# S5 scan states laid out in runs of two blocks, with a 17th row for the carry

## Chip, core and metric

The kernel runs on one core of one Trainium2 chip. The metric is device time in microseconds (us) of one execution; a single number for a kernel is the median of its runs.

## What is computed

The program is two trunk layers of a diffusion backbone over 2048 latent tokens and 256 context tokens, with 1024 channels. The change is in the second (odd) layer, in its bidirectional S5 branch: 512 channels in 32 groups of 16, each group with 64 complex states and two directions.

```python
def linear_scan(lam_bar, bu, h0, reverse):
    """h_t = lam_bar * h_{t-1} + bu_t along axis 1 (or reversed)."""

def s5_direction(u_lat, u_ctx, ...):          # context scan first, the latent scan starts from its end
    h_ctx = linear_scan(lam_bar, drive(u_ctx), None, reverse)
    h_end = h_ctx[:, 0] if reverse else h_ctx[:, -1]
    h_lat = linear_scan(lam_bar, drive(u_lat), h_end, reverse)
    return read(h_lat), ...

z = gelu(y_forward + y_backward + d_skip * u);  val, gt = split(z @ w_glu + b_glu);  out = val * sigmoid(gt)
```

Beside it the odd layer has a gated MLP branch: layer norm, a 128 x 128 mix of positions, and two gates, with its own input projections.

## The kernel before

Eight tokens are folded into one position by matrices computed ahead, so that the scan runs over 288 positions a direction: 32 of the context and 256 of the latent tokens. `middle` projects the input `u` of the branch band by band, copies it out of PSUM with ScalarE into `s` (L1430) and stores it in DRAM as `s_d`.

`s5_quarter` (L1617) then runs four times, each time for 8 of the 32 groups (below: a quarter). Its parts:

- **Drive.** For each of four group pairs `gp`, the position table `mi` and the input `U` are loaded, TensorE writes `pd` (L1634), and ScalarE copies it to the state tile `S` (L1636): 128 partitions x (2 directions, 2 parts (real, imaginary), 4 pairs, 288 positions), fp32.
- **Scan in blocks.** The 288 positions are 18 blocks of 16. VectorE steps through the 16 rows of all blocks at once: 15 steps of five instructions (L1655 to L1660), each step reading row i-1 and updating row i of 18 blocks, both directions and 8 part-and-pair rows. Three instructions have 288 elements a partition and two have 144. Neighbouring elements of a row are 16 floats (64 bytes) apart, since a block's positions are contiguous.
- **Carries.** 17 more steps of the same five lines, on 16 or 8 elements, take the last state of each block to the next.
- **Correction.** The carry, multiplied by the powers of the eigenvalue in the table `pa`, is added to the other 15 rows of 17 blocks: the forward direction on VectorE in 8 instructions of 1020 elements, the backward direction on POOL in 16 of 510 (L1697 to L1700 for both).
- **Output.** SyncE's queue brings `S` to `O` in another partition order (L1710). TensorE sums three matmuls a group (L1718 to L1720); ScalarE applies GELU (L1722), VectorE notes the maximum (L1723), and `z` goes to DRAM.

`S` has two buffers, `O` three. In program order the four quarters come first and then `odd_pair`, once for every 256 latent tokens, for the gated MLP; a compile-time planner orders the instructions of each engine by its own times, and so the pairs' work lies between that of the quarters. Each engine works off its list in order. In a pair, TensorE fills up to four PSUM banks `pu` (L181), and VectorE takes them: the layer-norm statistics of the first two (L1576), a row of small instructions for a reciprocal square root (L122 to L136), a gate (L1594) for the third and fourth, and a product (L1598). POOL multiplies `vc` (L1588) and `sy` (L1607). With all banks full, TensorE waits until VectorE gets to the gate.

After the quarters and six pairs come `glu_in`, `glu_z` and two further pairs, then `glu` (product `yg`, L1780) and `final` (the output projection).

Of the kernel before, what the change touches and what calls it, by code (L numbers as in the profile page):

```python
# [9 lines left out]
F32 = mybir.dt.float32  # L10
# [3 lines left out]
AF = mybir.ActivationFunctionType  # L14
OP = mybir.AluOpType
# [39 lines left out]
class Kern:  # L55
# [729 lines left out]
    def step(self):  # L785
        c = next(self.steps, (7, 0))
        if isinstance(c, tuple):
            self.ahead = c
        else:
            self.ahead = None  # L790
            self.credit = max(self.credit - c, -AHEAD)
# [573 lines left out]
    def middle(self, mw, w2, ow):  # L1365
        nc, I, tc = self.nc, self.I, self.tc
# [3 lines left out]
        gp = {k: self.gate_row(self.wop, k) for k in ("l0", "c0")}  # L1370
        ws = self.load_w(w2, I["w_in_odd"], 2560, 1536, 512)
        u_s = self.product(self.u_h, ws[2], 1.0)
# [9 lines left out]
        with self.pool_("midh", side="right") as pool:  # L1382
            for at, b in enumerate(MID_ORDER):
# [40 lines left out]
                if b == 3:  # L1424
                    mw.close()
                    self.s5a = mw.enter_context(self.pool_("s5a"))
                for j in range(4):
                    s = pool.tile([128, 8, n // 8], F32, name=self.name("s"), tag="s", bufs=1)
                    ps = self.mid_mm(ws, j, hs, n)
                    nc.scalar.activation(s.rearrange("p s n -> p n s"), ps.rearrange("p (n s) -> p n s", s=8), AF.Copy,  # L1430
                                         scale=u_s)
                    for at in ([32 + t0 // 8] if b < 4 else [0, 288]):
                        nc.sync.dma_start(self.s_d[j, :, :, at:at + n // 8], s)
                if b == 3:
# [182 lines left out]
    def s5_quarter(self, pool, pb, j):  # L1617
        nc = self.nc
        pa = pool.tile([128, 2, 2, 2, 4, 17], F32, name=self.name("pa"), tag="pa", bufs=2)
        nc.sync.dma_start(pa, self.pa_d[:, j].rearrange("p (a d r g i) -> p a d r g i", a=2, d=2, r=2, g=4))  # L1620

        S = pb.tile([128, 2, 2, 4, 288], F32, name=self.name("S"), tag="S", bufs=2)
        for gp in range(4):
            mi = pool.tile([128, 512], F32, name=self.name("mi"), tag="mi", bufs=2)
            nc.sync.dma_start(mi, self.min_d[4 * j + gp])
            U = pool.tile([128, 2, 320], F32, name=self.name("U"), tag="U", bufs=2)
            for gpar in range(2):
                nc.sync.dma_start(U[:, gpar, :], self.s_rows(j, 2 * gp + gpar, 0, 320))
            for d in range(2):
                ps = self.ps.tile([128, 2, 512], F32, name=self.name("pd"), tag="s", bufs=1)  # L1630
                for ri in range(2):
                    for gpar in range(2):
                        c = (2 * d + ri) * 128 + 64 * gpar
                        nc.tensor.matmul(ps[64 * gpar:64 * gpar + 64, ri, 0:288], mi[:, c:c + 64],  # L1634
                                         U[:, gpar, 32 * d:32 * d + 288], start=True, stop=True)
                nc.scalar.activation(S[:, d, :, gp, :], ps[:, :, 0:288], AF.Copy)  # L1636
        DS, RS = 8 * 288, 4 * 288
        t1 = pool.tile([128, 4 * 17 * 15], F32, name=self.name("t1"), tag="t1", bufs=1)
        t2 = pool.tile([128, 4 * 17 * 15], F32, name=self.name("t2"), tag="t2", bufs=1)

        def ap(off, dstep, n, step):
            return bass.AP(tensor=S.tensor, offset=S.offset + off, ap=[list(S.ap[0]), [dstep, 2], [288, 8], [step, n]])

        def half(off, dstep, n, step):
            return bass.AP(tensor=S.tensor, offset=S.offset + off, ap=[list(S.ap[0]), [dstep, 2], [288, 4], [step, n]])

        def tab(part):
            return pa[:, part]

        def step(cur, prev, ar, ai, n):  # L1650

            m = 16 * n
            x1 = t1[:, 0:m].rearrange("p (d q n) -> p d q n", d=2, q=8)
            x2 = t2[:, 0:m].rearrange("p (d q n) -> p d q n", d=2, q=8)
            nc.vector.tensor_tensor(x1, ap(*prev), ar, op=OP.mult)  # L1655
            nc.vector.tensor_tensor(x2, ap(*prev), ai, op=OP.mult)  # L1656
            nc.vector.tensor_tensor(ap(*cur), ap(*cur), x1, op=OP.add)  # L1657
            nc.vector.tensor_tensor(half(*cur), half(*cur), x2[:, :, 4:8], op=OP.subtract)  # L1658
            c2 = (cur[0] + RS,) + cur[1:]
            nc.vector.tensor_tensor(half(*c2), half(*c2), x2[:, :, 0:4], op=OP.add)  # L1660

        ar = [tab(p)[:, :, :, :, 16].rearrange("p d r g -> p d (r g)")[:, :, :, None].to_broadcast([128, 2, 8, 18])
              for p in range(2)]
        for i in range(1, 16):
            step((i, DS + 15 - 2 * i, 18, 16), (i - 1, DS + 17 - 2 * i, 18, 16), ar[0], ar[1], 18)
        a16 = [tab(p).rearrange("p d r g i -> p d (r g) i") for p in range(2)]

        def last(p):

# [1 line left out]
            return bass.AP(tensor=x.tensor, offset=x.offset + 15, ap=[list(x.ap[0]), [8 * 17 - 15, 2], [17, 8], [1, 1]])  # L1671

        ll = [last(0), last(1)]
        for k in range(1, 18):
            step((16 * k + 15, DS + (17 - k) * 16 - (16 * k + 15), 1, 1),
                 (16 * k - 1, DS + (18 - k) * 16 - (16 * k - 1), 1, 1), ll[0], ll[1], 1)
        for d in range(2):

            cur0 = d * DS + (16 if d == 0 else 1)
            car0 = d * DS + (15 if d == 0 else 16)  # L1680

            def v(off, q, i):
                return bass.AP(tensor=S.tensor, offset=S.offset + off,
                               ap=[list(S.ap[0]), [288, q], [16, 17], [1, 15] if i else [0, 15]])

            i0 = 0 if d == 0 else 1
            tb = [a16[p][:, d, :, None, i0:i0 + 15].to_broadcast([128, 8, 17, 15]) for p in range(2)]
            eng, m = (nc.vector, 4) if d == 0 else (nc.gpsimd, 2)
            if d == 0:
                x1, x2 = t1, t2  # L1690
            else:
                x1, x2 = [pool.tile([128, m * 17 * 15], F32, name=self.name("tp"), tag=f"tp{k}", bufs=1) for k in range(2)]
            x1, x2 = [x.rearrange("p (q b i) -> p q b i", q=m, b=17) for x in (x1, x2)]
            for ri in range(2):
                for q in range(0, 4, m):
                    cur = v(cur0 + ri * RS + q * 288, m, True)
                    eng.tensor_tensor(x1, v(car0 + ri * RS + q * 288, m, False), tb[0][:, q:q + m], op=OP.mult)  # L1697
                    eng.tensor_tensor(x2, v(car0 + (1 - ri) * RS + q * 288, m, False), tb[1][:, q:q + m], op=OP.mult)
                    eng.tensor_tensor(cur, cur, x1, op=OP.add)
                    eng.tensor_tensor(cur, cur, x2, op=OP.add if ri else OP.subtract)  # L1700
        T = pool.tile([128, 8, 128], F32, name=self.name("T"), tag="T", bufs=1)
# [2 lines left out]
                                                        [[240, 16], [32 * 240, 8], [1, 128]]))  # L1704
        for gp in range(4):

            O = pb.tile([128, 2, 2, 288], F32, name=self.name("O"), tag="O", bufs=3)
            for gpar in range(2):
                for ri in range(2):
                    nc.sync.dma_start(O[64 * ri:64 * ri + 64, gpar], S[64 * gpar:64 * gpar + 64, :, ri, gp, :])  # L1710
            for gpar in range(2):
                g = 2 * gp + gpar
                u = pool.tile([128, 256], F32, name=self.name("Uy"), tag="Uy", bufs=3)
                nc.sync.dma_start(u, self.s_rows(j, g, 32, 256))
                mo = pool.tile([128, 2, 144], F32, name=self.name("mo"), tag="mo", bufs=3)
                nc.sync.dma_start(mo, dap(self.mo_d, (8 * j + g) * 256 * 144, [[144, 128], [128 * 144, 2], [1, 144]]))
                ps = self.psg((128, 256))
                nc.tensor.matmul(ps, T[:, g, :], u, start=True, stop=False)  # L1718
                nc.tensor.matmul(ps, mo[:, 0, 16:144], O[:, gpar, 0, 31:287], start=False, stop=False)
                nc.tensor.matmul(ps, mo[:, 1, 0:128], O[:, gpar, 1, 1:257], start=False, stop=True)  # L1720
                z = pool.tile([128, 256], F32, name=self.name("z"), tag="z", bufs=3)
                nc.scalar.activation(z, ps, AF.Gelu_apprx_tanh)  # L1722
                nc.vector.tensor_reduce(self.zmax[:, 8 * j + g:8 * j + g + 1], z, axis=AX.X, op=OP.max,  # L1723
                                        apply_absolute_value=True)
                nc.sync.dma_start(dap(self.z_d, (j * 128 + 16 * g) * 2048, [[256, 8], [2048, 16], [1, 256]]), z)
# [34 lines left out]
    def glu(self, pool, zs, z0):  # L1760
# [3 lines left out]
        for b in range(4):  # L1764
            zh, zl = self.glu_z(pool, zs, b) if b else z0
            for j in range(4):
# [4 lines left out]
                for i, w in ((1, wg[1]), (0, wg[0])):  # L1771
# [5 lines left out]
                nc.scalar.activation(va, ps[0], AF.Identity, bias=bv[:, j:j + 1], scale=uvc)  # L1777
                nc.vector.scalar_tensor_tensor(va, th, 1.0, va, op0=OP.add, op1=OP.mult)
                y = pool.tile([128, 512], F32, name=self.name("yg"), tag="yg", bufs=2)
                nc.vector.tensor_tensor(y.rearrange("p (n t) -> p t n", t=8), va.rearrange("p (t n) -> p t n", t=8),  # L1780
                                        G.rearrange("p (n t) -> p t n", t=8), op=OP.mult)
                self.note_max(y, b, 4 + j)
                nc.sync.dma_start(self.yo_d[4 + j, :, 512 * b:512 * b + 512], y)

# [86 lines left out]
```

## Time and profile before

| | us |
|---|---|
| median of 3 runs | 2462.55 |
| lowest, highest | 2454.91, 2464.0 |
| the profiled execution | 2459.69 |
| its span in the trace | 2457.9 |
| TensorE busy | 2223.6 |
| VectorE (DVE) busy | 1625.8 |
| ScalarE (ACT) busy | 1047.0 |
| GpSimd (POOL) busy | 445.7 |

The span leaves 1.8 us of the profiled execution outside; that execution is 2.9 us below the median. Shares over the whole span are averages over very different stages. The four quarters lie between about 1700 and 2090 us of the span, and the window table and the instruction timelines of this stretch are what to read.

### The profile page before, as it was taken

The numbers are of one execution on the slowest core, as the hardware profiler recorded it, in microseconds if no ns is written. First come the engines' busy times: TensorE is split into PE (matmuls) and PEld (weight loads), VectorE is DVE, ScalarE is ACT, GpSimd is POOL, SyncE is SP. The second block draws the span as 40 slices with busy tenths as digits, with TensorE's granted clock in tenths as the row PEclk, the third lists the DMA queues.
The fourth block names the chain that finished last, engine by engine and source line by source line (L and its number), as shares of the span: only waits on it lengthen the run. The fifth ranks groups of instructions, "written<-read, shape, count | busy, mean of one in ns | idle before, by whom it ended". The sixth has DMA issues, their size and how long they took to land.

```text
span 2457.9 us, 43136 instructions
## 1 busy us (share of the span) xinstructions
PE 2223.6 (90%) x15860; PEld 1421.2 (58%) x15860; DVE 1625.8 (66%) x4343; ACT 1047.0 (43%) x2208; POOL 445.7 (18%) x533
## 2 busy tenths in 40 slices
PE   5999997998999999999878999978968787999998
PEld 2667784675766666666564566666534443544443
DVE  5888413466576666766686767751799998457555
ACT  4822232455556565555565555532211211244232
POOL 0123100122222222222340000000053154110000
PEclk8999998999999999999988999989989888999999
DMA  9845756224343343523433435552234532556332
GB/s 321 255 119 147 192 166 177 69 74 135 83 139 99 93 140 102 138 76 102 155 113 102 164 124 138 163 175 91 79 87 124 143 98 79 147 151 206 116 116 90
DMA packets 344165, 324.98 MB, mean 132 GB/s; under 512 B 93154, under 2 KB 290158, under 8 KB 343058
## 3 DMA queue, kind: packets, MB, share of 16 engines
q1 hardware_dynamic: 343842, 322.20, 44.1%
q8 instruction: 125, 2.05, 0.3%
q14 instruction: 86, 0.70, 0.1%
q10 hardware_dynamic: 112, 0.03, 0.0%
HBM read 210.10 MB, written 102.59 MB: 127 GB/s over the span
## 4 chain that ended last, share of the span: by engine, by line
PE 60%; DVE 22%; DMA 8%; issue 3%; ACT 3%; SPq 2%; POOL 1%; DVEq 0%; ACTq 0%; POOLq 0%
PE pg L181 36%; PE pu L181 6%; PE S L997 4%; PE PT L1016 4%; DVE S L1657 2%; PE pv L1030 2%; DVE t L1655 2%; DVE t L1656 2%; DVE S L1658 2%; DVE wl L190 1%; PE pa L331 1%; DMA wf<-in_w_in_even_dram 1%; DVE S L1660 1%; PE pv L1033 1%; DMA s_d<-s 1%
## 5 line engine op out<-in xcount | busy, mean ns | idle before, releaser
L181 PEld LDWEIGHTS <-wh 128*128 128x128 f16 x2944 | 280.0, 98 | 168.3 <-issue 10.8
L1000 DVE CUSTOM_DVE_ANT_0 P<-S,bias,slab 128x640 f32<-128x640 f32 (+2 forms) x216 | 193.6, 896 | 162.6 <-PE S L997 161.5
L189 ACT ACTIVATE ph<-PT 128x384 f16<-128x384 f32 (+1 forms) x408 | 172.6, 457 | 217.2 <-PE PT L1016 216.2
L181 PE MATMUL pu<-wh,h1p 128*128 128x512 f16 x768 | 191.2, 397 | 45.0 <-DVE Gs L1594 42.5
L181 PEld LDWEIGHTS <-h1p 128*128 128x128 f16 x1152 | 115.2, 101 | 192.4 <-issue 72.9
L949 POOL TENSOR_TENSOR bias<-G,masks 128x384 f32<-128x384 f32 (+1 forms) x144 | 152.6, 1060 | 349.6 <-DVE t L1000 326.9
L181 PEld LDWEIGHTS <-wl 128*128 128x128 f16 x1472 | 142.7, 100 | 116.2 <-issue 31.9
L190 DVE SCALAR_TENSOR_TENSOR pl<-PT,ph 128x384 f16<-128x384 f32 (+1 forms) x408 | 195.1, 508 | 13.9 <-ACT ph L189 12.5
L1002 ACT ACTIVATE P<-P,t 128x640 f32<-128x640 f32 (+2 forms) x216 | 181.2, 839 | 40.2 <-DVE t L1000 38.9
L181 PE MATMUL pg<-hh,wl 128*128 128x512 f16 (+1 forms) x800 | 183.6, 363 | 15.6 <-DVE stg L190 7.5
L181 PE MATMUL pg<-hl,wh 128*128 128x512 f16 (+1 forms) x800 | 181.9, 361 | 0.0
L181 PE MATMUL pg<-hh,wh 128*128 128x512 f16 (+1 forms) x800 | 180.6, 358 | 0.0
L181 PEld LDWEIGHTS <-yh 128*128 128x128 f16 x1088 | 106.5, 98 | 124.3 <-issue 0.8
L1016 PE MATMUL PT<-ident,P 128*128 128x128 f32 x1104 | 162.8, 277 | 11.5 <-DVE pl L190 9.6
L997 PEld LDWEIGHTS <-Q 128*128 128x128 f16 x1776 | 132.7, 99 | 62.7 <-issue 22.0
L997 PE MATMUL S<-K,Q 128*128 128x128 f16 (+1 forms) x1776 | 160.2, 234 | 1.8 <-DVE t L1000 1.7
L181 PE MATMUL pg<-wh,yl 128*128 128x512 f16 x544 | 133.1, 386 | 5.2 <-DVE yl L190 5.1
L1016 PEld LDWEIGHTS PT<-ident,P 128*128 128x128 f32 x1104 | 120.6, 142 | 20.7 <-issue 8.4
L1037 POOL TENSOR_TENSOR o<-o 128x64 f32<-128x64 f32 x216 | 73.3, 339 | 323.9 <-ACT o L1036 322.6
L181 PE MATMUL pg<-wh,yh 128*128 128x512 f16 x544 | 130.3, 379 | 0.0
L181 PE MATMUL pg<-wl,yh 128*128 128x512 f16 x544 | 130.2, 379 | 0.0
L156 DVE TENSOR_REDUCE t<-wf 128x1 f32<-128x1024 f32 x68 | 82.5, 1216 | 71.9 <-DMA wf<-in_w_in_odd_dram 25.4
(341 smaller groups left out, 4168.3 us busy)
## 6 DMA issues: line engine op xcount, KB each, us to landing
wada<-in_w_ada_dram SPq DMA_DIRECT2D x34, 512.0 KB
x<-in_x_dram SPq DMA_DIRECT2D x32, 512.0 KB
wf<-in_w_in_even_dram SPq DMA_DIRECT2D x28, 512.0 KB
V<-vs SPq DMA_DIRECT2D x192, 64.0 KB
K<-kd SPq DMA_DIRECT2D x96, 128.0 KB
wf<-in_w_in_odd_dram SPq DMA_DIRECT2D x20, 512.0 KB
Y<-ys SPq DMA_DIRECT2D x144, 64.0 KB
O<-S SPq DMA_DIRECT2D x64, 144.0 KB
```

Source lines behind the costliest of these rows:

```text
L156: nc.vector.tensor_reduce(m[:, i:i + 1], f, axis=AX.X, op=OP.max, apply_absolute_value=True)
L181: nc.tensor.matmul(ps, a(k), b(k), start=(n == 0), stop=(n == 3 * kb - 1))
L189: nc.scalar.activation(hi, src, AF.Copy, scale=scale)
L190: nc.vector.scalar_tensor_tensor(lo, src, scale, hi, op0=OP.mult, op1=OP.subtract)
L949: nc.gpsimd.tensor_tensor(q4(bv), gv, q4(masks[:, m0:m0 + 128 * nch]), op=OP.add)
L997: nc.tensor.matmul(S[:, at:at + m], u["q"], K[:, hl, off:off + m], start=(hl == 1), stop=(hl == 0))
L1000: nc.vector.tensor_tensor_reduce(P[:, 0:n], S[:, 0:n], u["B"][:, 0:n], u["negf"], 3.4e38, OP.add, OP.min, nm)
L1002: nc.scalar.activation(P[:, 0:n], P[:, 0:n], AF.Exp, bias=nm, scale=-1.0, accum_out=l)
L1016: self.nc.tensor.transpose(PT[:, c - a:c - a + 128], P[:, c:c + 128], self.ident)
L1030: nc.tensor.matmul(pv, ph[:, i * 128:(i + 1) * 128], vals[i][:, hd * 128:hd * 128 + 128], start=(i == 0), stop=False, skip_group_check=True)
L1037: nc.gpsimd.tensor_tensor(o["t"][:, hd * 64:(hd + 1) * 64], o2[:, 0:64], o2[:, 64:128], op=OP.add)
L1655: nc.vector.tensor_tensor(x1, ap(*prev), ar, op=OP.mult)
```

## The change

- `S` grows from 288 to 306 floats a row. Two neighbouring blocks share a run: 9 runs of 34 floats, 17 rows of 2, with the position in row r of block k at 34 (k // 2) + 2 r + k % 2. Row 0 (forward) or row 16 (backward) holds the state carried into the block.
- A scan step then covers 9 pairs of neighbouring floats for each of its 16 part-and-direction rows, still 288 and 144 elements. There are still 15 steps.
- The carry steps write into the new row: 16 steps and one copy in place of 17. The first carry is zero, set by POOL in 16 elements a quarter.
- The correction covers 18 blocks: 1080 and 540 elements for 1020 and 510. The powers are doubled into a tile `tw` (one buffer) by one ScalarE instruction a quarter of 1024 elements.
- The output matmuls read the state before each position as 8 runs of 32 floats; `O` and its transfers grow with `S`.
- Positions are put in the new order when `s` is written, by two ScalarE instructions a band of 512 in place of one, and put back in `glu` by two VectorE instructions of 256 elements in place of one of 512.

```diff
-                    nc.scalar.activation(s.rearrange("p s n -> p n s"), ps.rearrange("p (n s) -> p n s", s=8), AF.Copy,
-                                         scale=u_s)
+                    sv = s.rearrange("p s (b i k) -> p b k i s", i=16, k=2)
+                    pv = ps.rearrange("p (b k i s) -> p b k i s", k=2, i=16, s=8)
+                    for h in range(n // 256):
+                        nc.scalar.activation(sv[:, h], pv[:, h], AF.Copy, scale=u_s)
...
-        S = pb.tile([128, 2, 2, 4, 288], F32, name=self.name("S"), tag="S", bufs=2)
+        NS = 9 * 34
+        DS, RS = 8 * NS, 4 * NS
+        S = pb.tile([128, 2, 2, 4, NS], F32, name=self.name("S"), tag="S", bufs=2)
+        nc.gpsimd.memset(bass.AP(tensor=S.tensor, offset=S.offset, ap=[list(S.ap[0]), [DS + 8 * 34 + 33, 2], [NS, 8], [1, 1]]), 0.0)
...
-                nc.scalar.activation(S[:, d, :, gp, :], ps[:, :, 0:288], AF.Copy)
+                nc.scalar.activation(S[:, d, :, gp, :].rearrange("p r (b x) -> p r b x", x=34)[:, :, :, 2 - 2 * d:34 - 2 * d],
+                                     ps[:, :, 0:288].rearrange("p r (b x) -> p r b x", x=32), AF.Copy)
+        tw = pool.tile([128, 2, 2, 8, 32], F32, name=self.name("tw"), tag="tw", bufs=1)
+        nc.scalar.activation(tw.rearrange("p a d q (i k) -> p (a d q) i k", k=2),
+                             pa.rearrange("p a d r g i -> p (a d r g) i")[:, :, 0:16, None].to_broadcast([128, 32, 16, 2]),
+                             AF.Copy)
...
-            return bass.AP(tensor=S.tensor, offset=S.offset + off, ap=[list(S.ap[0]), [dstep, 2], [288, 8], [step, n]])
+        def rows(r, q):
+            o, dstep = 2 * r, DS + 32 - 4 * r
+            return bass.AP(tensor=S.tensor, offset=S.offset + o, ap=[list(S.ap[0]), [dstep, 2], [NS, q], [34, 9], [1, 2]])
...
-        for i in range(1, 16):
-            step((i, DS + 15 - 2 * i, 18, 16), (i - 1, DS + 17 - 2 * i, 18, 16), ar[0], ar[1], 18)
+        for r in range(2, 17):
+            step(lambda q: rows(r, q), lambda q: rows(r, q), lambda q: rows(r - 1, q), ar[0], ar[1], (9, 2))
...
-        for k in range(1, 18):
-            step((16 * k + 15, DS + (17 - k) * 16 - (16 * k + 15), 1, 1),
-                 (16 * k - 1, DS + (18 - k) * 16 - (16 * k - 1), 1, 1), ll[0], ll[1], 1)
+        nc.vector.tensor_copy(one(0, 1, 8), one(16, 0, 8))
+        for k in range(1, 17):
+            step(lambda q: one(0, k + 1, q), lambda q: one(16, k, q), lambda q: one(0, k, q), ll[0], ll[1], (1,))
...
-                               ap=[list(S.ap[0]), [288, q], [16, 17], [1, 15] if i else [0, 15]])
+                if row is None:
+                    return bass.AP(tensor=S.tensor, offset=S.offset + o + 2, ap=[list(S.ap[0]), [NS, n], [34, 9], [2, 15], [1, 2]])
+                return bass.AP(tensor=S.tensor, offset=S.offset + o + 2 * row, ap=[list(S.ap[0]), [NS, n], [34, 9], [0, 15], [1, 2]])
...
-                nc.tensor.matmul(ps, mo[:, 0, 16:144], O[:, gpar, 0, 31:287], start=False, stop=False)
-                nc.tensor.matmul(ps, mo[:, 1, 0:128], O[:, gpar, 1, 1:257], start=False, stop=True)
+                nc.tensor.matmul(pv, mo[:, 0, 16:144], ov[:, 0, 1:9, 0:32], start=False, stop=False)
+                nc.tensor.matmul(pv, mo[:, 1, 0:128], ov[:, 1, 0:8, 2:34], start=False, stop=True)
...
-                nc.vector.tensor_tensor(y.rearrange("p (n t) -> p t n", t=8), va.rearrange("p (t n) -> p t n", t=8),
-                                        G.rearrange("p (n t) -> p t n", t=8), op=OP.mult)
+                for h in range(2):
+                    c = slice(256 * h, 256 * h + 256)
+                    f = lambda t: t[:, c].rearrange("p (k i t) -> p k i t", k=2, t=8)
+                    nc.vector.tensor_tensor(f(y), va.rearrange("p (t b i k) -> p b k i t", t=8, b=2, k=2)[:, h], f(G), op=OP.mult)
```

## Rows read from the trace of the kernel before

**Rows 1.** The page: busy us, share of the span and instructions of each engine.

```profile
PE 2223.6 (90%) x15860; PEld 1421.2 (58%) x15860; DVE 1625.8 (66%) x4343; ACT 1047.0 (43%) x2208; POOL 445.7 (18%) x533
```

**Rows 2.** Windows: stretch, length, busy us (instructions) by engine, TensorE clock, DMA, GB/s.

```profile
1735.00:1797.00 62.00, 60.84 (x363) 32.22 (x362) 59.55 (x182) 14.12 (x26) 6.22 (x5) 1.00 0.26 82
1797.00:1825.00 28.00, 11.13 (x42) 4.42 (x41) 28.00 (x26) 0.69 (x1) 27.15 (x16) 0.78 0.26 63
1825.00:1883.00 58.00, 54.28 (x307) 33.70 (x306) 55.95 (x180) 15.44 (x30) 5.55 (x4) 0.93 0.52 149
...
2080.00:2273.00 193.00, 189.59 (x914) 95.79 (x913) 114.51 (x221) 72.09 (x101) 23.77 (x19) 0.99 0.57 166
```

**Rows 3.** Waits of 1690 to 2110 us: waiter, releaser, us in total, times, longest.

```profile
PE pu L181 <- DVE Gs L1594: 42.5, 7, 11.1
```

**Rows 4.** The page's chain that ended last: shares of the span by line.

```profile
PE pg L181 36%; PE pu L181 6%; PE S L997 4%; PE PT L1016 4%; DVE S L1657 2%; PE pv L1030 2%; DVE t L1655 2%; DVE t L1656 2%; DVE S L1658 2%; DVE wl L190 1%; PE pa L331 1%; DMA wf<-in_w_in_even_dram 1%; DVE S L1660 1%; PE pv L1033 1%; DMA s_d<-s 1%
```

**Rows 5.** Groups by line and shape, 1690 to 2100 us: count, busy us, mean ns, idle before.

```profile
L1657 DVE TENSOR_TENSOR S<-S,t 128x288 f32<-128x288 f32 x60 | 45.9, 765 | 1.0
L1655 DVE TENSOR_TENSOR t<-S,pa 128x288 f32<-128x288 f32 x60 | 41.7, 695 | 1.5 <-ACT S L1636 0.3
L1656 DVE TENSOR_TENSOR t<-S,pa 128x288 f32<-128x288 f32 x60 | 40.7, 679 | 0.0
...
L1658 DVE TENSOR_TENSOR S<-S,t 128x144 f32<-128x144 f32 x60 | 31.1, 518 | 1.2
...
L1660 DVE TENSOR_TENSOR S<-S,t 128x144 f32<-128x144 f32 x60 | 24.0, 401 | 0.8
...
L1656 DVE TENSOR_TENSOR t<-S,pa 128x16 f32<-128x16 f32 x68 | 12.1, 178 | 0.0
```

**Rows 6.** Timeline of VectorE: one scan step and the next one's start; start, us.

```profile
1754.37 0.64 DVE L1655 TENSOR_TENSOR t<-S,pa 128x288 f32<-128x288 f32 x1
1754.92 0.63 DVE L1656 TENSOR_TENSOR t<-S,pa 128x288 f32<-128x288 f32 x1
1755.59 0.67 DVE L1657 TENSOR_TENSOR S<-S,t 128x288 f32<-128x288 f32 x1
1756.30 0.41 DVE L1658 TENSOR_TENSOR S<-S,t 128x144 f32<-128x144 f32 x1
1756.74 0.41 DVE L1660 TENSOR_TENSOR S<-S,t 128x144 f32<-128x144 f32 x1
1757.18 0.64 DVE L1655 TENSOR_TENSOR t<-S,pa 128x288 f32<-128x288 f32 x1
```

**Rows 7.** Line L1697: count, duration ns min/median/max, first and last start, shape.

```profile
L1697 POOL TENSOR_TENSOR tp<-S,pa x16: 1089/2062/2102, 1796.7 to 2082.7; 128x510 f32<-128x510 f32 x16
L1697 DVE TENSOR_TENSOR t<-S,pa x8: 1220/1702/2192, 1796.6 to 2066.4; 128x1020 f32<-128x1020 f32 x8
```

**Rows 8.** Timeline of VectorE: a scan instruction while POOL runs its correction.

```profile
1813.47 1.46 DVE L1655 TENSOR_TENSOR t<-S,pa 128x288 f32<-128x288 f32 x1
```

**Rows 9.** Timelines: TensorE's matmuls of a statistics bank, and VectorE's reading of that bank.

```profile
1783.38 3.62 PE L181 MATMUL pu<-wh,h1p 128*128 128x512 f16 x16
...
1793.83 0.69 DVE L1576 BATCH_NORM_STATS2 t<-pu 128x6 f32<-128x512 f32 x1
...
1869.40 3.62 PE L181 MATMUL pu<-wh,h1p 128*128 128x512 f16 x16
...
1878.44 0.69 DVE L1576 BATCH_NORM_STATS2 t<-pu 128x6 f32<-128x512 f32 x1
```

**Rows 10.** Lines L1430 and L1780: count, duration ns min/median/max, starts, shapes.

```profile
L1430 ACT ACTIVATE s<-pg,slab x20: 685/1143/1174, 1406.2 to 1653.2; 128x512 f32<-128x512 f32 x16, 128x256 f32<-128x256 f32 x4
...
L1780 DVE TENSOR_TENSOR yg<-va,Gd x16: 1077/1095/1102, 2192.5 to 2274.5; 128x512 f32<-128x512 f32 x16
```

**Rows 11.** Timelines of POOL and SyncE's queue: `sy`, and the last transfer out of `S`.

```profile
1841.55 2.80 POOL L1607 TENSOR_TENSOR sy<-sy,Gs 128x512 f32<-128x512 f32 x2 [5.23 <-ACT sy L1606]
...
1842.80 0.61 SPq L1710 DMA_DIRECT2D O<-S  x1
```

## What the change should do

> **What bounds the kernel now.** Read first the page's busy shares [rows 1]: TensorE has 90% of the span, VectorE 66%. By that alone a VectorE edit would seem worth little. Then read the windows of the S5 stretch [rows 2]. From 1735 to 1797 us VectorE is busy 59.55 of 62 us and TensorE 60.84; in the 28 us that follow, VectorE is busy throughout, POOL for 27.15, and TensorE for only 11.13, at a granted clock of 0.78; from 1825 to 1883 VectorE is busy again for 55.95 of 58. This pattern repeats, once a quarter, until about 2080, after which TensorE is the full engine (189.59 of 193). The waits say who holds whom: TensorE waited 42.5 us for the gate L1594 on VectorE, seven times [rows 3]. The chain agrees: the scan lines L1655 to L1660 hold about 9% of the span on it [rows 4], some 220 us. So for four quarters VectorE's list sets the pace, TensorE idles at the end of each quarter, and after 2080 TensorE has a fixed amount of work. What VectorE saves in the quarters is saved at the end, as far as TensorE keeps up.
>
> **The scan steps.** These are 60 steps of five instructions, 183.4 us busy in all [rows 5]. An undisturbed step is 0.64, 0.63 and 0.67 us for the instructions of 288 elements and 0.41 twice for those of 144; the next starts 2.81 us after it [rows 6]. What would they cost at the rate of contiguous data? The nearest rows are an instruction of 1020 elements, contiguous in its rows, at 1.220 us when nothing holds it [rows 7], and one of 16 at 0.178 [rows 5]. Between them lie 1.042 us for 1004 elements: 1.04 ns an element and 0.16 us fixed. So 288 elements would take 0.46 us and 144 would take 0.31. At 64 bytes' step they take (0.64 - 0.16) / 288 = 1.66 ns an element. A step thus saves 0.18 + 0.17 + 0.21 + 0.10 + 0.10 = 0.76 us, if pairs of neighbouring floats run at the contiguous rate; 60 steps save 45.6. No row shows an operand in runs of two, so the bounds are 0 (the strided row) and 45.6 (the contiguous one). I take 45.6: a run of two halves the jumps, and a strided element costs 1.6 times a contiguous one, so one jump in two elements fits into the time that the second element gives.
>
> [...] No row of this trace shows the pair.
>
> **Carries.** One step of five instructions goes and one copy comes. At 0.178 us each [rows 5], which overlap partly, that is 0.5 us a quarter, -2 in all; bounds 0 and -3.
>
> **The correction.** 60 more elements on VectorE add 0.06 us to each of 8 instructions; 30 more on POOL, at 1.089 us for 510, add 0.06 to each of 16 [rows 7]. The two slow each other: POOL's median is 2.06 us against a least of 1.09. POOL fills the window of 28 us and VectorE's work of this time goes through between its instructions, so the window grows by between 16 x 0.06 = 1.0 and 6% of 28 = 1.7 us. I take 1.2 a quarter: +5. In the first three quarters it lies between the statistics and the gate for which TensorE waits; in the last one POOL's `sy` is queued behind it.
>
> **What TensorE can follow.** The first bank of statistics was full half way through the row of 16 matmuls, at 1785.2, and VectorE read it at 1793.83; in the second quarter 1871.2 and 1878.44 [rows 9]. So the slack is 8.6 and 7.2 us. VectorE would arrive 15 x 0.76 + 0.5 = 11.9 us earlier in the first quarter, with TensorE full until then: VectorE waits some 3.2. In the second, some 13 steps lie behind the last gate, 10.4 us with the carries, but TensorE's own start moves with the gate and with `vc`; I take a wait of 1.8. In the last two quarters the same reading gives no slack under 10 us, and I take 0. Together +5; bounds 0 and +15 (a loss of some 3.5 in each of four).
>
> **On ScalarE, the queues and in `glu`.** `s`: a band of 512 goes from 1.143 us to two of 0.685 [rows 10], +0.23 us in 16 places; most lie under TensorE, the last four on a chain of copies and stores: +0.5, bounds 0 and +3.6. `tw`: at (1.143 - 0.685) / 256 = 1.8 ns an element, 1.9 us of ScalarE a quarter, which is busy 15.44 of 58 us there [rows 2]; it waits for POOL's correction of the quarter before, and behind it in ScalarE's list stand `S` copies, gates and `vc`, needed by TensorE. ScalarE is nearly empty in the correction window (0.69 of 28), so I take 0; without that cover it is 1.9 x 4 = 7.6. The memset: a rival, below. `O` transfers: 6% more bytes, 144 to 153 KB, same count, same place in SyncE's queue; 0. The three matmuls of a group read 32 contiguous floats at a time in place of 256; 0, since 9 runs have 8 more jumps in 256 elements. `yg`: 1.095 us becomes two of 256 elements, at 0.43 (contiguous) to 0.59 (strided) each: -0.2 to +0.1 in 16 places, while TensorE is full; 0, bounds -4 and +2.
>
> **The sum.** -45.6 - 2 + 5 + 5 + 0.5 = -37 us. The profiled execution has 2459.7, so it would come to 2422.6. It lies 2.9 below the median of the runs; against the median, 2462.55, the forecast is 2425. One caution on the size: of the scan's mean durations, 3.06 us a step against 2.76 undisturbed, 0.30 x 60 = 18 us are waits beside POOL [rows 5, 6]; I keep them, though shorter instructions may meet POOL less.
>
> **Rivals.**
>
> *Pairs run no faster (slower).* Every second element still jumps; if that is what costs, the steps save nothing, and the carry of the correction, which was one float repeated, becomes a pair repeated 15 times and pays too. With r ns an element for pairs, the steps save 60 x 1152 x (1.66 - r) ns; the correction's first two lines lose 17,280 x (r - 1.04) ns on VectorE and as much on POOL, which hold one another, and the rest costs about 3.5 us. The signs change at r = 1.42. At r = 1.66 it is +21 + 3.5, some 2487 us; with POOL's half hidden, 2476. For it: no row shows a pair. Against it: the strided rate is 1.6 and not 2 or more times the contiguous one. At r between 1.2 and 1.42 it would be 2438 to 2462.
>
> *TensorE or the order becomes the bound.* If all four quarters can give no more than the least slack, 7.2 us, the gain is 28.8 - 5 = 24 and the time 2439. For it: TensorE was full for 60.84 of 62 us in the first scan [rows 2]. Against it: 16.9 us of each 28 us window are idle on TensorE, and the banks wait for VectorE there.
>
> *POOL's list.* The memset of a quarter's `S` waits until the transfers out of the same buffer, two quarters earlier, are through. The last of them was issued at 1842.80, while POOL began `sy` at 1841.55 [rows 11]. A memset put ahead of `sy` in POOL's list holds `sy`, and the transposes behind it on TensorE, for 3 to 4 us; this can come in two quarters: +7, 2432.
>
> *The lock with POOL.* A scan instruction in the correction window takes 1.46 us in place of 0.64 [rows 8]: it waits for POOL's. Two of the steps in each of three quarters lie there; if they gain nothing, 3 x 2 x 0.76 = 4.6 us go, 2430. [...]
>
> *More than forecast.* Without VectorE's waits for TensorE, and with half of the 18 us beside POOL gone, it is 37 + 5 + 9 = 51 us: 2411.
>
> **How the numbers follow.** The forecast, with the two small rivals that lie beside it (2415 to 2436): 0.58. More: 0.10. TensorE as bound (2436 to 2450): 0.14. Pairs at a rate between (2438 to 2462): 0.09. Pairs no faster (2462 to 2487): 0.09. A range from 2406 to 2451 leaves out the last case, most of the one before and a little at the low end. A measurement of this kernel can tell about 0.5%, 12.3 us, from no change: below 2450.2 is faster, above 2474.9 slower. Faster: 0.58 + 0.10 + 0.13 + 0.02 = 0.83; same: 0.11; slower: 0.06.
>
> **What the profile would show.** Right: L1655's successor at 0.46 us undisturbed and its half-size companion at 0.31, a step of about 2.05 us, the corrections of neighbouring quarters some 10 us closer together, TensorE's wait for the gate still there but its idle time smaller, and the stretch after the quarters unchanged in length. Wrong: 0.64 us for the pairs; or 0.46 with VectorE idle for TensorE in front of the statistics; or a correction whose first two lines grow by more than 6%; or POOL or ScalarE standing at the memset or at `tw` with `sy` or a gate behind it.

## The result, and the profile after

The changed kernel takes **2587.99 us** in the median (2583.30 to 2592.68), the kernel before 2461.51 beside it. The ratio is 1.0518, with a 95% interval of 1.0490 to 1.0547: **slower by 126 us**. The forecast was 2425 us, with a range of 2406 to 2451.

The scan itself did what was forecast: it became faster. A timeline of VectorE in the changed kernel (start, us; an undisturbed step), to set beside [rows 6]:

```profile
1745.56 0.46 DVE L1677 TENSOR_TENSOR t<-S,pa 128x288 f32<-128x288 f32 x1
1745.94 0.45 DVE L1678 TENSOR_TENSOR t<-S,pa 128x288 f32<-128x288 f32 x1
1746.42 0.46 DVE L1679 TENSOR_TENSOR S<-S,t 128x288 f32<-128x288 f32 x1
1746.92 0.31 DVE L1680 TENSOR_TENSOR S<-S,t 128x144 f32<-128x144 f32 x1
1747.15 0.30 DVE L1682 TENSOR_TENSOR S<-S,t 128x144 f32<-128x144 f32 x1
1747.48 0.46 DVE L1677 TENSOR_TENSOR t<-S,pa 128x288 f32<-128x288 f32 x1
```

From one step to the next it is 1.92 us, where it was 2.81. VectorE is also less busy over the whole span, 1580.6 us where it was 1625.8 [rows 1]. The page of the changed kernel, busy time by engine, and then TensorE, VectorE and TensorE's clock in 40 slices of the span (tenths):

```profile
PE 2243.7 (87%) x15860; PEld 1431.6 (55%) x15860; DVE 1580.6 (61%) x4343; ACT 1050.1 (41%) x2228; POOL 445.9 (17%) x537
...
PE   5998998999999999998789999882442899999998
...
DVE  5888313665676766665867677339997122358555
...
PEclk8999999999999999998889999895666999999999
```

The hole is in slices 28 to 31, some 1750 to 2005 us: the S5 quarters. VectorE is full there and TensorE nearly idle; afterwards it is the other way round. The window view (stretch, length, busy us and instructions by engine, granted clock, DMA share, GB/s), of the changed kernel:

```profile
1740.00:2090.00 350.00, 175.21 (x734) 96.18 (x735) 257.51 (x714) 42.87 (x81) 115.48 (x72) 0.70 0.38 101
2090.00:2420.00 330.00, 327.27 (x1692) 168.71 (x1691) 148.58 (x337) 98.73 (x152) 34.29 (x26) 1.00 0.33 99
```

and of the kernel before:

```profile
1740.00:2090.00 350.00, 285.89 (x1468) 156.20 (x1465) 335.21 (x834) 63.24 (x125) 135.22 (x84) 0.90 0.37 103
2090.00:2420.00 330.00, 321.05 (x1519) 154.82 (x1517) 185.49 (x445) 115.58 (x157) 16.62 (x12) 0.99 0.47 144
```

Up to 2090 us TensorE has run half as many instructions as before, 734 for 1468, and been busy 110.7 us less. Who holds it? The waits of TensorE, 1690 to 2110 us (waiter, releaser, us in total, times, longest):

```profile
PE pg L1743 <- DMA O<-S: 117.3, 4, 48.5
```

The wait for the gate on VectorE, 42.5 us [rows 3], is gone. In its place TensorE waits four times, once a quarter, for the corrected states that the transfers bring to `O`: nothing else stands in its list that it could do meanwhile. What used to stand there is the gated MLP. The first instruction of a pair on ScalarE, the gate `G` (count, duration in ns, first and last start), in the changed kernel:

```profile
L1555 ACT ACTIVATE G<-pg,slab x8: 682/687/687, 2021.9 to 2145.8; 128x512 f32<-128x512 f32 x8
```

and before:

```profile
L1552 ACT ACTIVATE G<-pg,slab x8: 682/687/689, 1714.2 to 1951.3; 128x512 f32<-128x512 f32 x8
```

All eight came beside the quarters; now the first starts 308 us later, when the quarters are through. So the question was not what the scan costs but why the pairs no longer lie between the quarters.

**The theory: 2,176 bytes.** The planner lets an instruction that writes a buffer wait for the last reader of whatever held those bytes. S5's buffers are laid from one end of SBUF, those of the pairs (`G`, `vc`, `Gs`, `sy`, `syT`) from the other. `G` has the lowest address of these. In the two built programs (bytes of a partition):

```
                         before    after
last O buffer ends at    133,920   141,888
G begins at              139,712   139,712
room between them          5,792   - 2,176
```

The growth of 7,968 can be added up from the diff: `S` 2 x 16 x 18 x 4 = 2,304, `O` 3 x 4 x 18 x 4 = 864, `t1` and `t2` 480, the two `tp` 240, `tw` 4,096; that is 7,984, and rounding takes off 16. With it the third `O` buffer covers `G` and the first bytes of `vc`, and it is last read in the last quarter.

**The rivals** of this theory (A): (B) the scan's own new waits (the zeroing on POOL, `tw` with its one buffer, the larger states) push the pairs back; (C) the planner's order is so touchy that any shift of addresses or names upsets it.

### The profile page after: what moved, and what is told of

The parts are those of the page before. It is cut to its first block, busy times and chain, and to the rows that moved or that the text cites. A ratio compares the mean times of both kernels' runs of the same rounds, so it can differ in the third digit from the quotient of the medians.

```text
span 2586.9 us, 43210 instructions
## 1 busy us (share of the span) xinstructions
PE 2243.7 (87%) x15860; PEld 1431.6 (55%) x15860; DVE 1580.6 (61%) x4343; ACT 1050.1 (41%) x2228; POOL 445.9 (17%) x537
## 4 chain that ended last, share of the span: by engine, by line
PE 68%; DVE 13%; DMA 6%; issue 3%; POOL 3%; ACT 3%; SPq 1%; DVEq 0%; ACTq 0%; POOLq 0%
PE pg L181 37%; PE pu L181 12%; PE S L997 4%; PE PT L1016 4%; PE pv L1030 2%; DMA wf<-in_w_in_even_dram 1%; PE pa L331 1%; DVE t L1677 1%; PE pv L1033 1%; DVE S L1679 1%; DVE S L1680 1%; DVE t L1678 1%; DVE wl L190 1%; DVE t L156 1%; POOL tp L1720 1%
## 5 line engine op out<-in xcount | busy, mean ns | idle before, releaser
L181 PE MATMUL pu<-wh,h1p 128*128 128x512 f16 x768 | 176.9, 379 | 3.3 <-ACT vc L1590 1.7
L1743 PE MATMUL pg<-O,mo 128*128 128x256 f32 x64 | 26.5, 505 | 118.2 <-DMA O<-S 117.3
```

Source lines behind the costliest of these rows:

```text
L181: nc.tensor.matmul(ps, a(k), b(k), start=(n == 0), stop=(n == 3 * kb - 1))
L1743: nc.tensor.matmul(pv, mo[:, 0, 16:144], ov[:, 0, 1:9, 0:32], start=False, stop=False)
```

## The experiments

Medians are in us; each ratio is against runs of the kernel before on the same chip (2459.14 for the first four runs, 2464.77 for the next four, 2459.72 for two, 2463.45 for the last).

**1 and 2: only bytes, on the kernel before.** An unused tile ahead of `S`; the two runs differ by 32 bytes.

```diff
+        pad = pool.tile([128, 1448], F32, name=self.name("pad"), tag="pad", bufs=1)
         S = pb.tile([128, 2, 2, 4, 288], F32, name=self.name("S"), tag="S", bufs=2)
```

```diff
+        pad = pool.tile([128, 1456], F32, name=self.name("pad"), tag="pad", bufs=1)
         S = pb.tile([128, 2, 2, 4, 288], F32, name=self.name("S"), tag="S", bufs=2)
```

> The kernel before with one unused tile of 5,792 bytes per partition ahead of S in S5's buffers; nothing reads or writes it, and no instruction is added. Theory A (memory): S5's buffers and those of the pairs (G, vc, Gs, sy, syT) grow towards one another from the two sides of SBUF, 5,792 bytes were free between them before, and the change took 7,968; G then shares addresses with the third O buffer and no pair can begin before the last quarter. This pad uses the free bytes up exactly, nothing overlaps, so the time is that of before, 2455 to 2470 us, and G's first ScalarE instruction still stands near 1714 us. Theory B (the changed scan's own waits: the zeroing on GpSimd, the doubled powers with one buffer, the bigger scan state) has nothing to do with memory and expects 2455 to 2470 too. Theory C (any shift of addresses or of names makes the instructions be ordered otherwise) expects a time that differs, by tens of us, in either direction.

> As the run before, with an unused tile of 5,824 bytes, 32 bytes more: G and the third O buffer now share 32 bytes per partition. Theory A: the pairs wait for the last quarter as in the changed kernel, G's first ScalarE instruction moves from about 1714 us to behind 2050 us, TensorE stands idle beside the scans, and the time is above that of the changed kernel, since the scan is still the slow one: 2588 plus some 40 to 80 us (four quarters at 86.6 in place of 67 us), 2600 to 2680 us. Theory B: 2455 to 2470 us, for no part of the change is in it. Theory C: no telling, but no reason for a time that differs from the pad of 5,792 by over 100 us.

Measured: 2462.65 (ratio 1.0011, 0.9996 to 1.0025) and **2638.24** (1.0731, 1.0715 to 1.0747). Without any instruction of the change, 32 bytes cost 176 us. In the first the gate is where it was (count, ns, first and last start):

```profile
L1552 ACT ACTIVATE G<-pg,slab x8: 681/687/689, 1718.0 to 1954.9; 128x512 f32<-128x512 f32 x8
```

In the second, its instruction on VectorE (L1553, right behind it) first starts at 2070.5, and TensorE's costliest wait of 1690 to 2110 us is that of the changed kernel, and longer, since this kernel has the old, slower scan:

```profile
L1553 DVE SCALAR_TENSOR_TENSOR G<-G,pg x8: 686/688/689, 2070.5 to 2194.1; 128x512 f32<-128x512 f32 x8
```

```profile
PE pg L1720 <- DMA O<-S: 171.6, 4, 60.6
```

So B is not needed for the jump, since nothing of the changed scan is in this kernel; whether it adds to it, runs 3 and 4 tell. C falls: 5,792 bytes moved nothing, and the jump comes within the 32 bytes in which the two sets of buffers meet.

**3 and 4: the whole change, with room.** Fewer buffers elsewhere in S5, nothing else.

```diff
-                mo = pool.tile([128, 2, 144], F32, name=self.name("mo"), tag="mo", bufs=3)
+                mo = pool.tile([128, 2, 144], F32, name=self.name("mo"), tag="mo", bufs=2)
-                z = pool.tile([128, 256], F32, name=self.name("z"), tag="z", bufs=3)
+                z = pool.tile([128, 256], F32, name=self.name("z"), tag="z", bufs=2)
```

```diff
-            O = pb.tile([128, 2, 2, NS], F32, name=self.name("O"), tag="O", bufs=3)
+            O = pb.tile([128, 2, 2, NS], F32, name=self.name("O"), tag="O", bufs=2)
```

> The whole change, with two buffers in place of three for mo and for z: 1,152 and 1,024 bytes less, the 2,176 by which the changed kernel's S5 buffers reached into G and vc. Nothing else is edited. Theory A: pairs and quarters interleave again and the prediction's sum comes to be tested: 2425 us, 2406 to 2451. Theory B: about 2588 us, since every part of the change is still there. Third possibility: the pairs interleave but something else of the change costs what the scan gains, 2455 to 2490 us.

> The whole change, with two buffers in place of three for O (4,896 bytes less, so S5 ends 2,720 bytes short of G). Theory A: as the run before, 2406 to 2451 us, a little later than it if a third O buffer was worth something (the DMAs that fill O then wait for the output matmuls of two groups back). Theory B: 2588 us or more.

Measured: **2422.15** (0.9855, 0.9840 to 0.9870) and **2415.09** (0.9822, 0.9806 to 0.9838). Taking away 2,176 bytes gives back 166 us, and the change is worth 37 us, as forecast (by the ratio 32 to 39). B falls with that, since every part of the change is still there. The first gate `G` starts at 1720.5 us, beside the quarters again. The windows of run 3:

```profile
1740.00:2090.00 350.00, 315.03 (x1669) 175.01 (x1666) 301.57 (x858) 76.56 (x150) 139.21 (x90) 0.96 0.44 121
2090.00:2420.00 330.00, 313.55 (x1472) 146.13 (x1470) 193.94 (x495) 113.81 (x149) 11.64 (x8) 0.98 0.43 138
```

TensorE does 29 us more in the stretch than before and 140 more than in the changed kernel.

**5 and 6: the same two edits on the kernel before.** Controls.

> The kernel before with two buffers in place of three for mo and for z, and nothing of the change: what that edit alone is worth, to set beside the run of the whole change with it. If the edit only makes room: 2455 to 2470 us, no difference from before. If fewer mo and z buffers hurt, some us more, and the change itself is then worth more than the 37 us between before and that run; if it gains for a reason of its own, the change is worth less.

> The kernel before with two buffers in place of three for O, and nothing of the change. The changed kernel with two O buffers took 2415 us, 7 less than with two mo and z buffers. If the two-buffer O is itself what gains those 7 us (the instructions are ordered otherwise): 2450 to 2458 us. If the 7 us come only together with the changed scan: 2455 to 2470 us.

Measured: 2463.49 (1.0000, 0.9989 to 1.0011) and 2465.85 (1.0010, 0.9996 to 1.0023). On the kernel before, which has room, the edits gain nothing; what runs 3 and 4 gain over it is the change's.

**10: room made in another way.** `tw` in the buffer of `T`, which has the same size; three buffers of everything.

```diff
-        tw = pool.tile([128, 2, 2, 8, 32], F32, name=self.name("tw"), tag="tw", bufs=1)
+        tw = pool.tile([128, 2, 2, 8, 32], F32, name=self.name("tw"), tag="T", bufs=1)
```

> The whole change, with the doubled powers tw in the buffer of the tile T (the two have one size, 4,096 bytes), so S5 ends 1,920 bytes short of G with three buffers of everything; tw now waits until the output matmuls of the quarter before have read T, and T is loaded once the correction has read tw. Memory theory: 2406 to 2451 us. If the waits between tw and T cost much: the upper end of it, or above.

Measured: 2414.59 (0.9810, 0.9790 to 0.9830). Three ways of making room all bring the time back into the forecast's range. Why two of them are 7 us better than the third is open; the instructions stand in other orders in all three.

**7: is a microsecond of scan a microsecond of time?** Run 3, with one multiply of every long step run once more.

```diff
             nc.vector.tensor_tensor(x1, prev(8), ar, op=OP.mult)
+            if len(shape) == 2:
+                nc.vector.tensor_tensor(x2, prev(8), ar, op=OP.mult)
             nc.vector.tensor_tensor(x2, prev(8), ai, op=OP.mult)
```

> The changed kernel with two mo and z buffers, and each of the 60 long scan steps runs one of its multiplies once more (into the tile that the next multiply writes), so 60 more VectorE instructions of 288 elements, 0.46 us each where GpSimd is still and 0.54 to 0.58 us in the mean: 28 to 35 us of VectorE. Theory: the time of the scans stands on the path, and a us of scan is about a us of time (the prediction gave back some 8 of 45 us to waits for TensorE): 2422 plus 22 to 35, 2444 to 2457 us. Rival: with the changed scan TensorE has become the bound in this stretch, and the extra work hides: 2422 to 2430 us.

Measured: 2437.77 (0.9906, 0.9884 to 0.9928), 15.6 more than run 3 by the medians and 12.5 by the ratios (0.0051 of 2460): between the two expectations, so neither is right as put. VectorE is busy 22.4 us longer between 1700 and 2470 us (528.3 for 505.9); 0.6 to 0.7 of that comes out as time. Going from before to run 3 it was 45.0 us of VectorE (550.9 to 505.9) for 37.0 of time, 0.82. The steps themselves took 39.4 us more (143.0 to 182.4, more than the 28 to 35 expected); the reciprocal square roots took some 12 us less, because in this run's order 3 of their instructions met POOL's correction and in run 3 15 did. So most of a microsecond of VectorE's busy time still reaches the end, not all of it; TensorE alone is not the bound.

**8: what POOL's correction costs VectorE.** Run 3, without POOL's half of the correction; the backward direction's states then lack the carry.

```diff
-            for ri in range(2):
+            for ri in range(2 if d == 0 else 0):
```

> The changed kernel with two mo and z buffers, without GpSimd's correction: its 64 instructions of 540 elements are left out, so the states of the backward direction lack the carry of the blocks before. Theory: the 60 long steps take 143 us in place of 120 us (60 times three of 0.46 and two of 0.31) because GpSimd's correction holds them up at their memory: without it their means fall to 0.46 and 0.31, and the time falls by 15 to 30 us, to 2392 to 2407 us; VectorE's own correction (1.95 us in the mean for 1080 elements) shrinks a little too. Rival: the means above 0.46 come from other traffic (transfers, ScalarE's copies), GpSimd's correction is off the path, and the time stays within 5 us of 2422.

Measured: **2373.33** (0.9645, 0.9620 to 0.9670), 48.8 us less than run 3: the direction was right, the size more than half as much again as the most that was expected. Groups of VectorE, 1690 to 2110 us (count, busy us, mean ns), in run 3:

```profile
L1679 DVE TENSOR_TENSOR S<-S,t 128x288 f32<-128x288 f32 x60 | 29.2, 486 | 0.8
...
L1721 DVE TENSOR_TENSOR S<-S,t 128x1080 f32<-128x1080 f32 x8 | 17.0, 2127 | 0.0
...
L122 DVE TENSOR_SCALAR rs<-t,slab 128x2 f32<-128x2 f32 x7 | 4.2, 595 | 0.1
```

and in run 8:

```profile
L1679 DVE TENSOR_TENSOR S<-S,t 128x288 f32<-128x288 f32 x60 | 30.8, 514 | 1.0
...
L1721 DVE TENSOR_TENSOR S<-S,t 128x1080 f32<-128x1080 f32 x8 | 10.2, 1274 | 0.0
...
L122 DVE TENSOR_SCALAR rs<-t,slab 128x2 f32<-128x2 f32 x8 | 1.8, 226 | 0.1
```

The long steps gave back 11 us (143.0 to 131.9), about half of the 23 that were expected, and not everywhere: L1679 did not fall. The rest is POOL's `vc` and `sy`: counted in this trace, 27 of the 300 instructions of the long steps run beside one of these, at 0.92 us in the mean, and the other 273 take 0.39, as undisturbed ones do. What was not expected in this size: VectorE's own correction falls from 62.5 to 40.8 us. And the small instructions of the reciprocal square root, which stand before the gate, lose some 13 us between them (L122 is one), though run 7 shows that another order alone can spare 12 of these. The rival, that POOL's correction is off the path, falls. That POOL's 27 us a quarter no longer stand before the output matmuls is part of the gain too; this run does not part the two.

**9 and 11: the whole correction on VectorE**, on the changed kernel (where it also frees the two `tp`, 4,320 bytes, and so makes the room) and on the kernel before.

```diff
-            eng, m = (nc.vector, 4) if d == 0 else (nc.gpsimd, 2)
-            if d == 0:
+            eng, m = nc.vector, 4
+            if True:
                 x1, x2 = t1, t2
```

> The whole change with three buffers of everything, and GpSimd's half of the correction given to VectorE, in eight more instructions of 1080 elements per quarter; the two tiles tp (4,320 bytes) go, which makes more room than the 2,176 bytes that were wanting. Memory theory: pairs and quarters interleave. From the run without GpSimd's correction: VectorE takes 1.27 us for 1080 elements where GpSimd is still and 1.95 beside it, so all 64 of its instructions cost 81.5 us where 32 cost 62.5, and the 60 long steps get back 11 us: 8 us more of VectorE, and GpSimd's 27 us per quarter are off the path to the output matmuls. Expected 2400 to 2430 us, likeliest 2412. Rival: VectorE, which is 98% busy between 1800 and 2000 us, is the bound, and the 8 us more come out as such: 2428 to 2440 us.

> The kernel before, nothing of the change, with GpSimd's half of the correction given to VectorE (16 instructions of 1020 elements per quarter in place of 8, GpSimd's tiles gone). The same edit took the changed kernel, once it had room, from 2415 or 2422 to 2396 us. If GpSimd's correction holds VectorE up in the old layout too: VectorE alone takes 1.22 us for 1020 elements (the shortest of before), 64 of them 78 us where 32 took 60, the 60 long steps fall from 183 us towards 60 times three of 0.64 and two of 0.41, 164 us, so about even on VectorE, and GpSimd's 27 us per quarter off the path: 2440 to 2455 us. Rival: the old step's strided reads don't suffer from GpSimd, VectorE only gets 18 us more: 2465 to 2480 us.

Measured: **2395.56** (0.9736, 0.9722 to 0.9751) and 2447.14 (0.9939, 0.9921 to 0.9957). Run 9 is a complete kernel, faster than before by 64 us and than the changed one by 192; it went below its expected range. Its 64 correction instructions take 1.27 to 1.31 us in the mean of each line, about what an undisturbed one does; here is one line of them (count, ns min/median/max):

```profile
L1719 DVE TENSOR_TENSOR t<-S,tw x16: 1269/1274/1285, 1780.2 to 2019.6; 128x1080 f32<-128x1080 f32 x16
```

VectorE's busy time over the span was expected to rise by 8 us and fell by 9 (1576.3 in run 3, 1567.2), for the reciprocal square root again (13 us less, as in run 8). The same edit gives the kernel before 16 us, as expected, so it helps either layout; its long steps fell less than was worked out, from 183 to 177 us. With the change it gives 19 to 27 over the three kernels with room (runs 3, 4 and 10).

## Why the prediction was wrong, point by point

**The step that failed** stands in the part on ScalarE, the queues and `glu`, and in front of it: growing tiles were costed by the bytes that they move ("`O` transfers: 6% more bytes ... 0") and by the elements that they add, and nowhere by the bytes that they occupy. The whole sum then rested on the pairs staying between the quarters, which no sentence examined. The rival on the order asked whether TensorE would be the bound, not whether its work could still be placed there. Slower by 126 us lay outside the range and, being no case, outside the chances; the 0.06 for slower was for another mechanism.

It could not have been seen in the trace, which shows no addresses: [rows 2] and [rows 3] show the pairs beside the quarters, not that 5,792 bytes made it so. It could have been seen in the code. `S`, `O`, `t1`, `t2`, `tp` and `tw` are all in the diff, and the sum of their growth, some 8 KB, is to be set against what is free between the pools.

Given room, the steps of the sum can be compared with run 3, whose only difference from the changed kernel is the room:

| step | forecast, us | run 3 against before, us | from |
|---|---|---|---|
| 60 long steps | -45.6 | -40.4 | busy 183.4 to 143.0 |
| carries | -2 | -3.1 | busy 62.4 to 59.3, with the copy |
| correction on VectorE | +5, both engines | +2.7 | busy 59.8 to 62.5; POOL's 109.4 to 108.8 |
| VectorE waits for statistics | +5 | +3.3 | wait 17.1 to 20.4, 1690 to 2420 us |
| `s` | +0.5 | not told apart | |
| total | -37 | -37.0 | medians 2459.14 to 2422.15 |

- **Pairs at the contiguous rate** was right: 0.46 and 0.31 us were worked out, 0.45 to 0.46 and 0.30 to 0.31 measured. The rival at 0.64 us is out. That one jump in two elements fits into the time of the second element was the author's estimate; the rows show how long the instructions take, not why.
- **The steps gave 5 us less**, because what their means have above the undisturbed step, the waits beside POOL, grew from 18 us to 60 x (2.38 - 1.98) = 24 us and did not shrink (55 of the 300 instructions ran beside POOL's in run 3, 49 before): the caution in the prediction named the place, and half of "more than forecast" had the sign wrong.
- **The correction** cost half of what was taken; POOL's half did not grow at all.
- **TensorE's wait for the gate** fell from 42.5 us to 25.1, and stayed the largest, as "what the profile would show" had it.
- **POOL's list**: in run 3 POOL stood before the zeroing for transfers, 2.9 us once and 1.8 once, a little less than the rival's 3 to 4 twice. In the changed kernel it was 14.8 and 13.4 us.
- **`tw`** took 1.06 us a quarter, not the 1.9 worked out. ScalarE stood before it for POOL's correction once, for 12.0 us, in run 3, and 84.9 us in three waits in the changed kernel.
- **The output matmuls** with runs of 32 cost nothing more: 0.38 us in the median of 64 before and in run 3 (L1719 and L1743). Two of a group's three matmuls read so, in 8 runs; the prediction's "three" and "9 runs" are slips that change nothing.
- **`yg`** in two halves: 17.9 us for 17.5, against bounds of -4 and +2.
- **The sum had no term** for the reciprocal square roots. VectorE's busy time over the span fell by 49.5 us (1625.8 to 1576.3), the table's rows of busy time by 40.8. Some 8 of the rest are theirs: 15 of their instructions met POOL's correction in run 3, 25 before.

That these terms (-37.5) and the total agree to half a microsecond is in part luck: they are busy times and waits of one execution each, by run 7 not every microsecond of them reaches the end, and the 8 us that have no row are not among them. Runs 4 and 10, with the same scan, are 7 us faster.

## What to carry over

A tile that grows is paid for in bytes as well as in time: before costing its instructions, add up what all grown and new tiles occupy and compare it with the free room up to the pool on the other side; if the sum is larger, some later buffer inherits a wait for the last reader of an earlier one, and a planner like this one moves everything behind it. When TensorE goes idle beside a full VectorE after an edit that made VectorE faster, look first for the instruction that moved furthest (here `G`, by 308 us) and ask what its destination shares. And work given to POOL beside VectorE was not free here (46 us of VectorE's busy time in run 8): take the time that VectorE's instructions gain without it off what POOL takes over.

## What the hardware showed beside this

- **POOL beside VectorE took about as much from VectorE as it did for it, or more.** POOL's half of the correction took 109 us of POOL in run 3; without it VectorE's instructions were 46 us shorter (1576.3 to 1530.2 us busy over the span), while VectorE did that half in 41 us (run 9: 82.5 us for both halves, 40.8 for one in run 8). Of the 46, 13 are the reciprocal square roots, and how many of these meet POOL hangs on the order (run 7). With the whole correction on VectorE, VectorE was less busy in both layouts: 1567.2 us against 1576.3 to 1586.9 (runs 3, 4 and 10), and 1614.4 against 1625.8 (run 11 and before). The 1080-element instructions show it one by one: L1721 takes 1.27 us in the mean without POOL's correction (run 8) and 2.13 with it (run 3). Where the two engines hold each other up, at their memory or elsewhere, no run shows.
- **Instructions of two elements suffer most in proportion, when they meet POOL.** L122, two elements a partition, takes 0.23 us in the mean in run 8 and 0.60 in run 3; of L124, as small, the longest takes 1.11 in run 3 and 0.17 in run 8. POOL's correction instructions take 1.6 to 1.8 us in the mean of each line in run 3. In run 7, which has the correction too, the eight of L122 take 0.22 in the mean. In the kernel before, the four of L130 that ran beside POOL's correction took 1.08 us in the mean and the other 14 0.15, 7 times less; for 288 elements (L1656) it was 1.12 for six and 0.63 for 54, 1.8 times.
- **The granted clock was low where TensorE stood idle**: 0.70 in the mean between 1740 and 2090 us in the changed kernel, where TensorE was busy for half of the time, 0.96 in run 3; from 2090 to 2420 us it was 1.00 and 0.98. Within the hole, from 1760 to 1800 us, TensorE ran nothing but the start of one matmul (0.18 us), and the clock was 0.50. The same `pd` matmuls took 0.53 us in the mean in the changed kernel and 0.43 in run 3.
